# An encoder block on one core: the first head pair's bias and values loaded in the value stage, and value weights' low parts made on VectorE

## The chip, the cores and the metric

The kernel runs on one core of one Trainium2 chip. The metric is the device time of one execution in microseconds (us). Engines are called as the profile calls them: PE (TensorE, matrix products; PEld is its weight load), DVE (VectorE), ACT (ScalarE), POOL (GpSimd), and SP (SyncE), whose queue issues the transfers between HBM and the on-chip memory. PSUM is the memory into which PE writes, in eight banks.

## The reference

One layer of an encoder over 1024 positions of width 1024, all in float32. A conditioning vector gives six rows (shift, scale and gate for two halves); what matters here is the first half:

```
ada = silu(c) @ w_ada + b_ada          # six rows of 1024
h   = RMSNorm(x) * (1 + scale1) + shift1
[qA|kA|vA|qB|kB|vB|gA|gB] = h @ w_in   # widths 512 x 6, 1024 x 2
A: dilated window attention, patterns (128,1), (512,4), (2048,16) on the same q, k, v,
   merged per position by their softmax denominators, with a relative bias; 8 heads of 64
B: 2-D neighbourhood attention, 8 x 16 window, learned bias; 8 heads of 64
m = sigmoid(gA)*(oA @ w_branch_dil) + sigmoid(gB)*(oB @ w_branch_na);  x += gate1 * (m @ w_out)
```

After that come the feed-forward half (up projection, depthwise convolution, gated product, down projection) and a last norm, which the change doesn't touch.

## The kernel before, in words

Every product is done in a split form: an operand is copied by ACT to a rounded high part (`hi`), the rest (`lo`) is formed by a subtraction on POOL or DVE (`split`, line 54), and three matmuls hi*hi, hi*lo, lo*hi are summed in PSUM (`product`, line 74).

*The opening* (lines 385 to 460) takes the first 512 positions (x[0]). While its squares are summed, `warm` (line 207) keeps PE going with products of the identity into the PSUM tile `first`. Then follow four quarters q: `piece_bias` takes a quarter of shift and scale, `modulate` makes h for two of eight k tiles (DVE, ACT, DVE, by the two PSUM staging tiles `pcol` and `first`), PE adds them to the first q and k products and to the value products `pv`, and DVE sums the rows of `w_ada` for the next quarter (`ada_rows`, line 157), which PE then sums over partitions (`ada_sums`, tile `pada`). In the last quarter the second pair of value weights is loaded and split, with both low parts on POOL (line 424); the tile set is `vwh`, `vwl`. The squares of the second half of positions are divided over the quarters 2 and 3.

*The value stage* (lines 480 to 505, and 530) makes 24 value products `v_product` of 24 matmuls each, into three PSUM tiles `pv`. For each, `v_out` (line 244) lets ACT copy the result into a staging tile `vs`, of which there are three, and SP stores it to HBM (`vas`, `vbc`). Beside them run DVE's row sums over `wada` tiles (`row_pairs`), seven loads ahead, and copies from HBM to HBM which put the values in the order of the attention's blocks (`va_chunks`, and later `vb_chunks` for branch B).

*The attention of branch A* (`attend_dil`, line 555) starts with three things that come from HBM: the mask `lnm` (line 772, once), the bias `bt` of each head (lines 563 and 564; POOL adds the mask to its second part, line 565), and the values of the head, four transfers by `va_load` inside `v_tile` (lines 507 and 520), which ACT and POOL then split. For each of four residues r, PE makes scores into one of two tiles `S`, DVE adds the bias and takes the minimum (line 575), ACT takes the exponential, PE transposes, ACT and DVE split, and PE multiplies with the values into `O`.

*Order and memory.* Up to line 506 the order of the instructions on each engine is as written (`manual_schedule`). Everything after is put in order by a planner which works with a model of times, and it can put later instructions into gaps of the written order: the first score tile of head 0 and the second pair's q products are done among the value products. Pools are taken from a stack; `sm_pool`, which holds mask, bias, values and softmax tiles, is taken after `work` (the value weights and staging tiles, `adapool` and `early` (the `wada` tiles, row sums and squares) are released, and lies over their memory. A tile waits until what lay in its place was last read.

The lines that carry the two spots:

```
            if q == 3:
                v_w.append(v_split(v_load(0, 1), (pool, pool)))      # 424
    ...
            if q == 2:
                accs = sq_accs()
                square(x[1], accs, range(3), dve)                    # 435
    ...
        vs = work.tile([128, 256], FT, name="vs", bufs=3)            # 245
        act.activation(vs, p, AF.Copy)
```

Of the kernel before, what the change touches and what calls it, by code (L numbers as in the profile page):

```python
# [28 lines left out]
def hybrid_encoder(tc, xT, c, w_ada, small, w_in, p1_bias, p23_bias, na_bias, ln2_mult, ident, w_br, w_out,  # L29
# [8 lines left out]
    def f(ap):  # L38
        return ap.bitcast(FT)
# [73 lines left out]
    adapool = tc.alloc_tile_pool(name="ada", bufs=1, reuse_waits="tile")  # L113
    work = tc.alloc_tile_pool(name="start", bufs=2, reuse_waits="tile")
    ps_n = tc.alloc_tile_pool(name="psn", bufs=1, space=PSUM, reuse_waits="tile")
# [128 lines left out]
    def v_out(br, hv, st, p):  # L244
        vs = work.tile([128, 256], FT, name="vs", bufs=3)
        act.activation(vs, p, AF.Copy)  # L246
        sp.dma_start((va_s, vb_c)[br][st * 128:st * 128 + 128, hv * 256:hv * 256 + 256], vs)

    sig = work.tile([128, KT], FT, name="sig", bufs=1)
    act.activation(sig, cs, AF.Sigmoid)  # L250
# [134 lines left out]
    with tc.manual_schedule(engines={e.engine for e in (sp, act, dve, pool, pe)}):  # L385
# [29 lines left out]
        ada_sums([(wt[0][0], ones)], pa)  # L415
        warm(4, first[:, :128], True)
        stage[0] = ps_n.tile([128, 512], FT, name="pcol")
# [3 lines left out]
        for q in range(4):  # L421
            ks = range(2 * q, 2 * q + 2)
            if q == 3:
                v_w.append(v_split(v_load(0, 1), (pool, pool)))
            piece_bias(q, pa)
            modulate(x[0], 0, ks, pb)
            qk_products(ks)
            if q < 3:
                ada_rows(wt[q + 1], range(6))
            if q == 0:  # L430
                qk_split(1, (dve, dve))
                v_split(v_raw, (dve, dve), slice(4, 8), v_w[0])
            if q == 2:
                accs = sq_accs()
                square(x[1], accs, range(3), dve)
            if q == 3:
                square(x[1], accs, range(3, 8), dve)
            v_products(0, (0, 1), ks)
            if q < 3:
                pa = ada_sums([(wt[q + 1][t], cs[:, t:t + 1]) for t in (6, 7)], stop=False)  # L440
                ada_sums([(wt[q + 1][0], ones)], pa)
            v_products(0, (2, 3), ks)
# [23 lines left out]
        def row_pairs(n0, n1):  # L466
            for n in range(n0, n1):
# [9 lines left out]
                if n + 7 < len(pairs):  # L477
                    rows[n + 7] = pair_load(*pairs[n + 7])

        for n, (br, hv, st) in enumerate(v_steps[:19]):  # L480
            if n == 4:
# [20 lines left out]
            if n == 17:  # L502
                act.activation(sig, cs, AF.Exp)
            if n == 18:
                ada_bias(36, ada_sums([(sums.pop(9), ones)]))
        dve.scalar_tensor_tensor(am2, ada[:, 32:40], 1.0, g_ffn, OP.add, OP.mult)
    def va_load(head, vr):
        cc = slice(64 * head, 64 * head + 64)
        sp.dma_start(vr[:, 0:8], va_s.rearrange("(t p) n -> p t n", p=128)[:, :, cc])
        sp.dma_start(vr[:, 8:15], va_b[1:8].rearrange("j p n -> p j n")[:, :, cc])  # L510
        for x_, j in ((0, 0), (64, 8)):
            sp.dma_start(vr[x_:x_ + 64, 15], va_b[j, 0:64, cc])

# [5 lines left out]

    def v_tile(load, head, parts):  # L520

        vv = sm_pool.tile([128, 16, 128], FR, name="vv")
        lo = vv[:, :, 64:128]
        load(head, f(lo))
        for m, cs_ in parts:
            act.activation(vv[:m, cs_, 0:64], f(lo[:m, cs_]), AF.Copy)  # L526
            pool.tensor_tensor(lo[:m, cs_], f(lo[:m, cs_]), f(vv[:m, cs_, 0:64]), OP.subtract)  # L527
        return vv
# [3 lines left out]
    work.release()  # L532
    adapool.release()
    early.release()
    ps_s.release()
# [3 lines left out]
    ps_a = tc.alloc_tile_pool(name="psa", bufs=2, space=PSUM, reuse_waits="tile")  # L539
    sm_pool = tc.alloc_tile_pool(name="sm", bufs=2, reuse_waits="tile")  # L540

# [13 lines left out]
    def attend_dil(pr, qk, work):  # L555
# [3 lines left out]
        for i in range(2):  # L559
            head = 2 * pr + i  # L560
            a = slice(64 * i, 64 * i + 64)
            bt = sm_pool.tile([128, 896], FT, name="bias", bufs=2)
            sp.dma_start(bt[:, 0:512], p1_bias[head])
            sp.dma_start(bt[:, 512:896], p23_bias[head])
            pool.tensor_tensor(bt[:, 512:896], bt[:, 512:896], lnm, OP.add)
            vv = v_tile(va_load, head, ((128, slice(0, 16)),))

# [127 lines left out]
    def attend_na(pr, qk, work):  # L695
        qs, ks, kl, qb = qk
        oT = work.tile([128, S], FT, name="u1")
        for i in range(2):
# [3 lines left out]
            st = work.tile([128, 2, 8], FT, name="stb")  # L702
            vv = v_tile(vb_load, head, ((96, slice(0, 4)), (128, slice(4, 12)), (96, slice(12, 16))))
            col = 0
# [65 lines left out]
    with tc.tile_pool(name="at", bufs=2, reuse_waits="tile") as work:  # L770
        lnm = sm_pool.tile([128, 384], FT, name="lnm", bufs=1)
        sp.dma_start(lnm, ln2_mult)
# [685 lines left out]
```

## Time and profile before

| | |
|---|---|
| runs | 1565.9, 1569.3, 1570.37 us; median 1569.3 |
| profiled execution | 1566.2 us, of which the span of its instructions is 1564.4 us |
| PE busy | 1509.5 us, 96% of the span |
| DVE, ACT, POOL busy | 1024.4, 805.8, 801.8 us |
| granted clock of PE, mean | 0.982 of full speed |
| opening, value stage, first head pair | about 0 to 62, 62 to 174 and 174 to 260 us |

A row of a timeline has the start in us from the span's start, the duration in us, the engine, the line of the kernel, the operation, output <- input with partitions x elements, how many such instructions follow one another, and in brackets the idle time of the engine before and what ended it. SPq is the queue of SP; the time of a transfer there is that of its issue, not of its landing. A row of waits has the waiting engine, tile and line, what it waited for, then the total in us, the number of times and the longest. A row of stretches has its bounds, its length, the busy time (and count) of PE, PEld, DVE, ACT and POOL, the clock granted to PE (1.00 is full speed), the share of the DMA engines and GB/s.

### The profile page before, as it was taken

The numbers are of one execution on the slowest core, as the hardware profiler recorded it, in microseconds if no ns is written. First come the engines' busy times: TensorE is split into PE (matmuls) and PEld (weight loads), VectorE is DVE, ScalarE is ACT, GpSimd is POOL, SyncE is SP. The second block draws the span as 40 slices with busy tenths as digits, with TensorE's granted clock in tenths as the row PEclk, the third lists the DMA queues.
The fourth block names the chain that finished last, engine by engine and source line by source line (L and its number), as shares of the span: only waits on it lengthen the run. The fifth ranks groups of instructions, "written<-read, shape, count | busy, mean of one in ns | idle before, by whom it ended". The sixth has DMA issues, their size and how long they took to land. (4 is left out here: it accounts for less than half of the span.)

```text
span 1564.4 us, 22094 instructions
## 1 busy us (share of the span) xinstructions
PE 1509.5 (96%) x8012; PEld 1291.5 (83%) x8012; DVE 1024.4 (65%) x1874; ACT 805.8 (52%) x1448; POOL 801.8 (51%) x500
## 2 busy tenths in 40 slices
PE   8999799999999999999999888999999999999998
PEld 7899788888887998888888767888888887788787
DVE  6686266676756665535625888766666667877775
ACT  4432366666766677643335454444444446575542
POOL 1242243444337566411256858666666665679621
PEclk9899899999999999999999999999999999999999
DMA  9458522223133453557734212322222223533313
GB/s 352 164 201 292 156 73 73 81 77 93 51 90 111 141 138 104 184 187 238 228 128 149 74 54 81 108 81 81 81 82 90 86 74 136 182 114 121 115 54 109
DMA packets 114421, 196.87 MB, mean 126 GB/s; under 512 B 40200, under 2 KB 61576, under 8 KB 114312
## 3 DMA queue, kind: packets, MB, share of 16 engines
q1 hardware_dynamic: 114040, 195.20, 38.0%
q8 instruction: 63, 1.03, 0.3%
q14 instruction: 46, 0.38, 0.1%
q10 hardware_dynamic: 272, 0.26, 0.1%
HBM read 158.73 MB, written 42.47 MB: 129 GB/s over the span
## 5 line engine op out<-in xcount | busy, mean ns | idle before, releaser
L56 POOL TENSOR_TENSOR wlo<-wraw,whi 128x1024 fp32r<-128x1024 f32 (+2 forms) x78 | 179.9, 2307 | 284.1 <-ACT whi L55 275.1
L79 PE MATMUL pj<-h,whi 128*128 128x512 f32 x448 | 180.5, 403 | 3.8 <-ACT h L202 2.2
L80 PE MATMUL pj<-h,whi 128*128 128x512 f32 x448 | 179.4, 400 | 0.3 <-DVE h L204 0.3
L81 PE MATMUL pj<-h,wlo 128*128 128x512 f32 x448 | 178.8, 399 | 0.0
L56 POOL TENSOR_TENSOR wsl<-big,wsh 128x1024 fp32r<-128x1024 f32 (+1 forms) x45 | 109.3, 2432 | 50.6 <-ACT wsh L55 50.6
L1144 DVE SCALAR_TENSOR_TENSOR big<-wc,sm,big 128x256 f32<-128x256 f32 (+1 forms) x132 | 115.0, 919 | 17.3 <-ACT big L1138 17.2
L55 ACT ACTIVATE whi<-wraw 128x1024 fp32r<-128x1024 f32 (+2 forms) x81 | 81.3, 1003 | 87.0 <-PE pj L80 25.9
L338 POOL TENSOR_SCALAR kl<-kl 64x512 fp32r<-64x512 f32 x32 | 63.8, 1994 | 80.4 <-DVE kl L336 78.1
L79 PEld LDWEIGHTS pj<-h,whi 128*128 128x128 f32 x448 | 85.3, 190 | 20.6 <-ACT ks L337 3.4
L80 PEld LDWEIGHTS pj<-h,whi 128*128 128x128 f32 x448 | 85.4, 191 | 15.9 <-DVE h L204 1.1
L81 PEld LDWEIGHTS pj<-h,wlo 128*128 128x128 f32 x448 | 85.2, 190 | 15.0
L575 DVE CUSTOM_DVE_ANT_0 P<-S,bias 128x256 f32<-128x256 f32 x128 | 52.3, 420 | 53.7 <-PE S L622 31.9
L576 ACT ACTIVATE P<-P,st 128x256 f32<-128x256 f32 x128 | 64.3, 503 | 39.3 <-DVE st L575 38.7
L1144 DVE SCALAR_TENSOR_TENSOR big<-pj,sm,big 128x512 f32<-128x512 f32 x132 | 67.9, 564 | 16.1 <-ACT big L1138 16.1
L56 POOL TENSOR_TENSOR wsl<-wraw,wsh 128x768 fp32r<-128x768 f32 (+1 forms) x23 | 50.1, 2178 | 47.7 <-ACT wsh L55 47.7
L1138 ACT ACTIVATE big<-wc,sm 128x512 f32<-128x512 f32 x44 | 35.8, 816 | 74.5 <-DVE wc L961 45.6
L239 PE MATMUL pv<-vwh,h 128*128 128x256 f32 x256 | 73.7, 288 | 0.4 <-ACT vs L246 0.4
L240 PE MATMUL pv<-vwl,h 128*128 128x256 f32 x256 | 72.5, 283 | 0.0
L241 PE MATMUL pv<-vwh,h 128*128 128x256 f32 x256 | 72.5, 283 | 0.0
L527 POOL TENSOR_TENSOR vv<-vv 96x256 fp32r<-96x256 f32 (+2 forms) x32 | 41.0, 1294 | 59.3 <-ACT vv L526 59.1
L55 ACT ACTIVATE wsh<-big 128x1024 fp32r<-128x1024 f32 (+1 forms) x45 | 44.9, 1002 | 35.4 <-POOL big L913 18.3
L1170 ACT ACTIVATE big<-big 128x1024 f32<-128x1024 f32 x22 | 23.3, 1060 | 76.6 <-DVE big L1144 76.6
(379 smaller groups left out, 4923.7 us busy)
## 6 DMA issues: line engine op xcount, KB each, us to landing
wraw<-w_in SPq DMA_DIRECT2D x36, 512.0 KB, 3.5
wada<-w_ada SPq DMA_DIRECT2D x31, 512.0 KB, 7.1
big<-w_up SPq DMA_DIRECT2D x22, 512.0 KB, 5.0
wraw<-w_up SPq DMA_DIRECT2D x22, 512.0 KB, 3.7
as<-big SPq DMA_DIRECT2D x22, 512.0 KB, 3.0
big<-as SPq DMA_DIRECT2D x22, 512.0 KB, 8.1
wraw<-w_down SPq DMA_DIRECT2D x24, 384.0 KB, 4.2
gs<-gs SPq DMA_DIRECT2D x32, 256.0 KB, 2.5
```

The lines of the kernel that those rows point to most:

```text
L55: act.activation(hi, raw, AF.Copy)
L56: lo_eng.tensor_tensor(lo, raw, f(hi), OP.subtract)
L79: pe.matmul(psum, whi[:, k0 + k], mhi, start=k == 0, stop=False)
L80: pe.matmul(psum, whi[:, k0 + k], mlo, start=False, stop=False)
L81: pe.matmul(psum, wlo[:, k0 + k], mhi, start=False, stop=k == n - 1)
L239: pe.matmul(p, hhi, hi[:, k], start=fresh and k == 0, stop=False, skip_group_check=True)
L240: pe.matmul(p, hhi, lo[:, k], start=False, stop=False, skip_group_check=True)
L241: pe.matmul(p, hlo, hi[:, k], start=False, stop=k == KT - 1, skip_group_check=True)
L338: pool.tensor_scalar(ll[b], f(ll[a]), 1.0, None, OP.mult)
L575: dve.tensor_tensor_reduce(pp, d, bias, -1.0, BIG, OP.add, OP.min, mi)
L576: act.activation(pp, pp, AF.Exp, bias=mi, scale=-1.0, accum_out=li)
L1144: dve.scalar_tensor_tensor(y[:, dst], src, wt, y[:, dst], OP.mult, OP.add)
```

## The change

The mask, and bias and values of heads 0 and 1, are loaded at the end of the written order, behind the store of the nineteenth value product and ahead of the last five, by `dil_loads`; `attend_dil` takes these (`loads.pop(0)`), and calls `dil_loads` itself for later heads. `v_tile` no longer loads. For that `sm_pool` is taken earlier, over `adapool` and `early` only; `work` is moved to the other side of the memory, `vs` has two tiles and not three, and the small tile `sig` becomes one of the weight pool's `rs` tiles. In the opening the second value weights are loaded and split in quarter 2, with both low parts on DVE, after DVE's row sums of that quarter; all eight squares of the second half come in quarter 3; and the third `warm` has twelve products and not four.

```
-    work = tc.alloc_tile_pool(name="start", bufs=2, reuse_waits="tile")
+    work = tc.alloc_tile_pool(name="start", bufs=2, side="right", reuse_waits="tile")
...
-        vs = work.tile([128, 256], FT, name="vs", bufs=3)
+        vs = work.tile([128, 256], FT, name="vs", bufs=2)
...
-    sig = work.tile([128, KT], FT, name="sig", bufs=1)
+    sig = wpool.tile([128, KT], FT, name="rs", bufs=2)
...
-        warm(4, first[:, :128], True)
+        warm(12, first[:, :128], True)
...
-            if q == 3:
-                v_w.append(v_split(v_load(0, 1), (pool, pool)))
+            if q == 2:
+                v_raw1 = v_load(0, 1)
             piece_bias(q, pa)
             modulate(x[0], 0, ks, pb)
             qk_products(ks)
...
             if q == 2:
+                v_w.append(v_split(v_raw1, (dve, dve)))
+            if q == 3:
                 accs = sq_accs()
-                square(x[1], accs, range(3), dve)
-            if q == 3:
-                square(x[1], accs, range(3, 8), dve)
+                square(x[1], accs, range(8), dve)
...
+        def v_raw(load, head):
+            vv = sm_pool.tile([128, 16, 128], FR, name="vv")
+            load(head, f(vv[:, :, 64:128]))
+            return vv
+
+        def dil_loads(head):
+
+            bt = sm_pool.tile([128, 896], FT, name="bias", bufs=2)
+            sp.dma_start(bt[:, 0:512], p1_bias[head])
+            sp.dma_start(bt[:, 512:896], p23_bias[head])
+            return bt, v_raw(va_load, head)
...
-                act.activation(sig, cs, AF.Exp)
+                act.activation(wpool.tile([128, KT], FT, name="rs", bufs=2), cs, AF.Exp)
...
+        adapool.release()
+        early.release()
+        sm_pool = tc.alloc_tile_pool(name="sm", bufs=2, reuse_waits="tile")
+        lnm = sm_pool.tile([128, 384], FT, name="lnm", bufs=1)
+        sp.dma_start(lnm, ln2_mult)
+        loads = [dil_loads(head) for head in range(2)]
...
     for br, hv, st in v_steps[19:]:
         v_out(br, hv, st, v_product(st, v_w[br, hv]))
     work.release()
-    adapool.release()
-    early.release()
...
-            bt = sm_pool.tile([128, 896], FT, name="bias", bufs=2)
-            sp.dma_start(bt[:, 0:512], p1_bias[head])
-            sp.dma_start(bt[:, 512:896], p23_bias[head])
+            bt, vv = loads.pop(0) if loads else dil_loads(head)
             pool.tensor_tensor(bt[:, 512:896], bt[:, 512:896], lnm, OP.add)
-            vv = v_tile(va_load, head, ((128, slice(0, 16)),))
+            vv = v_tile(vv, ((128, slice(0, 16)),))
...
-        lnm = sm_pool.tile([128, 384], FT, name="lnm", bufs=1)
-        sp.dma_start(lnm, ln2_mult)
```

More of the change, by code (lines that the diff above doesn't have):

```diff
@@ L478, in row_pairs, with va_load @@
                     rows[n + 7] = pair_load(*pairs[n + 7])
+        def va_load(head, vr):
+            cc = slice(64 * head, 64 * head + 64)
+            sp.dma_start(vr[:, 0:8], va_s.rearrange("(t p) n -> p t n", p=128)[:, :, cc])
+            sp.dma_start(vr[:, 8:15], va_b[1:8].rearrange("j p n -> p j n")[:, :, cc])
+            for x_, j in ((0, 0), (64, 8)):
+                sp.dma_start(vr[x_:x_ + 64, 15], va_b[j, 0:64, cc])
+        def v_raw(load, head):
[7 more added lines that the diff above has]
+            return bt, v_raw(va_load, head)
         for n, (br, hv, st) in enumerate(v_steps[:19]):
@@ L506, in hybrid_encoder @@
         dve.scalar_tensor_tensor(am2, ada[:, 32:40], 1.0, g_ffn, OP.add, OP.mult)
[L507 to L512, printed above, removed]
+        adapool.release()
[4 more added lines that the diff above has]
+        loads = [dil_loads(head) for head in range(2)]
     def vb_load(head, vr):
@@ L518, in vb_load, with v_tile @@
             sp.dma_start(vr[:16 * n, 4 * cb:4 * cb + 4], vb_s[cb].rearrange("(g p) n -> p g n", g=4)[:, :, cc])
-    def v_tile(load, head, parts):
-        vv = sm_pool.tile([128, 16, 128], FR, name="vv")
+    def v_tile(vv, parts):
         lo = vv[:, :, 64:128]
-        load(head, f(lo))
         for m, cs_ in parts:
@@ L539, in hybrid_encoder @@
     ps_a = tc.alloc_tile_pool(name="psa", bufs=2, space=PSUM, reuse_waits="tile")
-    sm_pool = tc.alloc_tile_pool(name="sm", bufs=2, reuse_waits="tile")
     def finish_o(po, dst):
@@ L702, in attend_na @@
             st = work.tile([128, 2, 8], FT, name="stb")
-            vv = v_tile(vb_load, head, ((96, slice(0, 4)), (128, slice(4, 12)), (96, slice(12, 16))))
+            vv = v_tile(v_raw(vb_load, head), ((96, slice(0, 4)), (128, slice(4, 12)), (96, slice(12, 16))))
             col = 0
```

## The prediction

> **What bounds it now.** I read the busy table and then the waits of TensorE, over the whole span (total, times, longest).
>
> ```profile
> PE 1509.5 (96%) x8012; PEld 1291.5 (83%) x8012; DVE 1024.4 (65%) x1874; ACT 805.8 (52%) x1448; POOL 801.8 (51%) x500
> ```
>
> ```profile
> PE S L591 <- DVE st L575: 7.6, 1, 7.6
> PE pbc L106 <- DVE rs L100: 5.1, 2, 4.3
> PE pj L949 <- DVE T1lo L895: 3.0, 1, 3.0
> PE pada L148 <- DVE wada L164: 2.9, 1, 2.9
> ```
>
> TensorE (PE) is busy 96% of the span, so what can be won is its idle time and its slow clock. Its longest single wait, 7.6 us, is at the first attention scores; 2.9 us more are lost in the opening at the conditioning sums. The change touches exactly the code around these two. The stretches before, in and after the first wait (PE and its clock are the columns to read; the others are PEld, DVE, ACT, POOL, then DMA), and then the timeline of that place:
>
> ```profile
> 165.00:173.40 8.40, 8.40 (x56) 7.37 (x54) 0.00 (x0) 0.83 (x3) 0.00 (x0) 1.00 0.39 119
> 173.40:181.00 7.60, 0.07 (x1) 0.00 (x0) 1.10 (x4) 1.47 (x2) 3.33 (x2) 0.80 0.86 215
> 181.00:190.50 9.50, 8.20 (x44) 7.37 (x44) 5.36 (x22) 8.07 (x22) 5.71 (x3) 0.62 0.77 207
> ```
>
> ```profile
> 154.27 0.95 PE L148 MATMUL pada<-ones,sq 128*128 128x1 f32 x8
> 157.81 0.53 SPq L247 DMA_DIRECT2D vbc<-vs  x1
> ...
> 173.51 0.53 SPq L247 DMA_DIRECT2D vbc<-vs  x1
> 174.14 0.38 SPq L772 DMA_DIRECT2D lnm<-ln_mult  x1
> 179.56 0.99 POOL L565 TENSOR_TENSOR bias<-bias,lnm 128x384 f32<-128x384 f32 x1 [2.75 <-DMA bias<-p_bias]
> 180.59 0.42 DVE L575 CUSTOM_DVE_ANT_0 P<-S,bias 128x256 f32<-128x256 f32 x1 [5.00 <-POOL bias L565]
> 181.07 0.58 PE L591 MATMUL S<-ks,qs 128*128 128x256 f32 x1 [7.60 <-DVE st L575]
> 181.90 1.06 ACT L526 ACTIVATE vv<-vv 128x1024 fp32r<-128x1024 f32 x1 [7.03 <-DMA vv<-vab]
> ```
>
> The chain is plain: head 0's mask and bias are issued only at 174.1, behind the last store of values; they land at 179.56, GpSimd adds, VectorE takes the scores, and PE gets a free score tile at 181.07. Its clock, 1.00 before, is 0.62 until 190.5. The memory of these tiles lies over pools of the conditioning stage, last read near 155.2 (the sums at 154.27), and over the value stage's own pool, which the change moves to the other side.
>
> **The change part by part.**
>
> *The early loads.* Nothing is added: the mask, and six transfers a head, move from 174.14 to the end of the written order, behind the nineteenth store (157.81). Head 0's bias was there at 179.56 and its values at 181.90, 5.4 and 7.8 us after the first issue. From 158.4 that makes 163.8 and 166.2, or 170.9 and 173.3 if all wait the 7.1 us more that a loaded queue shows below; PE now has work without them until 173.4. So the 7.6 us go. Behind it, 8.20 busy us at a clock of 0.62 are 5.1 at full rate: up to 9.5 - 5.1 = 4.4 us lie in the stretch to 190.5. The chain score, softmax, transpose, product is still there for the first tiles, so I take 2.5 of them (bounds 0 and 4.4): -10.1 us. What was hidden: SP now issues thirteen transfers, at some 0.5 us, 6.5 us in all, ahead of the last five stores and of the copies of the other branch's values. Those copies are wanted four head pairs later and cost nothing; the stores hold a staging tile, and I put 0.5 us on them (0 to 3: three products can run on in PSUM).
>
> *VectorE takes the low parts.* The opening's third quarter:
>
> ```profile
> 47.00 5.16 POOL L56 TENSOR_TENSOR vwl<-wraw,vwh 128x1024 fp32r<-128x1024 f32 x2 [23.53 <-ACT vwh L55]
> 35.94 3.90 DVE L164 SCALAR_TENSOR_TENSOR wada<-wada,cs 128x512 f32<-128x512 f32 x5
> 45.63 4.33 DVE L164 SCALAR_TENSOR_TENSOR wada<-wada,cs 128x512 f32<-128x512 f32 x3
> 50.00 3.50 DVE L164 SCALAR_TENSOR_TENSOR wada<-qb,cs,wada 128x512 f32<-128x512 f32 x2
> 53.42 1.48 DVE L182 TENSOR_TENSOR sq<-sq,mt 128x512 f32<-128x512 f32 x2
> 53.55 1.86 PE L148 MATMUL pada<-ones,wada 128*128 128x1 f32 x8 [2.94 <-DVE wada L164]
> 55.46 0.16 DVE L255 TENSOR_TENSOR ada<-pada,sm 128x4 f32<-128x4 f32 x1 [0.56 <-PE pada L148]
> 56.64 0.69 ACT L202 ACTIVATE h<-pcol,ada 128x512 fp32r<-128x512 f32 x1 [8.77 <-DVE pcol L201]
> 57.99 0.61 PE L79 MATMUL pj<-h,whi 128*128 128x512 f32 x1
> 59.58 2.29 DVE L182 TENSOR_TENSOR sq<-sq,mt 128x512 f32<-128x512 f32 x3 [0.21 <-ACT mt L180]
> 66.60 1.84 PE L93 MATMUL pcol<-ones,sq 128*128 128x1 f32 x16
> L56 DVE TENSOR_TENSOR wlo<-big,whi x1: 1225/1225/1225, 873.4 to 873.4; 128x1024 fp32r<-128x1024 f32 x1
> ```
>
> While GpSimd makes the two low parts (47.0 to 52.2), VectorE's five row sums take 4.33 + 3.50; the five of the quarter before, with GpSimd idle, took 3.90. So 3.9 us are lost beside GpSimd, and with it idle they end at 45.63 + 3.90 = 49.5. PE was done with its earlier products at 53.55 - 2.94 = 50.6, so its wait is gone; its eight need some 1.0 (half of the sixteen at 66.60) and end near 51.7. VectorE's two low parts cost 2 x 1.225 and end at 52.0; the bias that waited until 55.46 comes at 52.0. PE's twelve value products (53.55 + 1.86 to 57.99 now, 2.7 with its slow clock) run from 51.7 to 54.4, and the first h (56.64 + 0.69, so 1.9 us after the bias at 55.46) is there at 53.9. So 57.99 becomes 54.4: -3.6 us. Bounds: -2.0 if the moved weights land or are copied late (GpSimd starts on them at 47.0 now, so their copies are in time for 49.5), -4.6 with a warm clock. On SP the second value weights keep their place, since nothing is issued between the old and the new spot. The two square additions (1.48 us) move behind the next products; the squares end at 61.87 now and the sums on PE start at 66.60, so cover is 4.7 us: nothing, and 1.5 us if it were gone.
>
> *Twelve warming products.* The first quarter:
>
> ```profile
> 19.68 1.14 PE L210 MATMUL pv<-idt 128*128 128x128 f32 x8
> 21.73 0.75 DVE L201 SCALAR_TENSOR_TENSOR pv<-h,am,pbc 128x512 f32<-128x512 f32 x1
> 23.00:27.00 4.00, 4.00 (x10) 2.84 (x10) 3.86 (x7) 0.94 (x3) 0.47 (x1) 0.50 1.04 395
> 32.20 0.16 DVE L255 TENSOR_TENSOR ada<-pada,sm 128x4 f32<-128x4 f32 x1 [1.46 <-PE pada L148]
> ```
>
> Each is two matmuls, so sixteen come on top of eight that took 1.14: 2.3 us, to 23.1. They write the PSUM tile that VectorE's second modulation (21.73) also writes, so that may start 1.4 us later. VectorE has 1.46 us of slack at 32.20, which covers it. PE's clock was 0.50 from 23 to 27, ten matmuls; at best that half is saved. I take 0, bounds -1.5 and +1.0. On this the Trainium skill ("TensorE: Matmul & The Clock Gate", "What's actually happening") says that the clock opens after a busy window of some 3.4 us; by that rule, with 20.8 (19.68 + 1.14) to 24.2 filled it would open one window earlier and the sum would be some 1.6 us lower, an estimate from that page. By that rule the trace agrees, in that the clock was at half after a stretch with PE partly idle; no run here has the window filled.
>
> *Two staging tiles for the stores, not three.* This speaks against the change.
>
> ```profile
> DMA to landing us min/median/max: 6.7/7.1/7.5
> 118.10 0.39 ACT L246 ACTIVATE vs<-pv 128x256 f32<-128x256 f32 x1 [2.11 <-DMA vas<-vs]
> 125.12 0.38 ACT L246 ACTIVATE vs<-pv 128x256 f32<-128x256 f32 x1 [6.63 <-DMA vas<-vs]
> 125.56 0.38 PE L239 MATMUL pv<-vwh,h 128*128 128x256 f32 x1 [0.36 <-ACT vs L246]
> 132.39 0.40 PE L80 MATMUL pj<-h,whi 128*128 128x512 f32 x1
> 132.62 0.40 PE L79 MATMUL pj<-h,whi 128*128 128x512 f32 x1
> 161.02 0.39 ACT L246 ACTIVATE vs<-pv 128x256 f32<-128x256 f32 x1 [2.42 <-PE pv L241]
> ```
>
> (The first row is of the staging tile.) A store lands 7.1 us after its issue, and ScalarE already waits for the third store back. With two tiles it waits for the second: the copy of 118.10 moves to the landing that released 125.12. A product takes 2.42 + 0.39 = 2.8 us (161.02) and waits for the copy three before it. The one before 125.56 ended at 125.2, so it began at 122.4; it could now not begin before that copy ends at 125.5: 3.1 us of PE. Later ones meet the next pair's projections, 96 matmuls 0.23 apart (132.39 to 132.62), 22 us that PE can do meanwhile. I take +3.0; bounds 0 (the queue, not the tile, may be what is late) and 10 (no projections in the gaps: of the same lag at the three or so later places where ScalarE waits).
>
> The sigmoid in another pool's tile, and the pool's side, add no instruction: 0.
>
> **Sum.** -10.1 + 0.5 - 3.6 + 0 + 3.0 = -10.2 us. The profiled execution took 1566.2 us, so 1556.0 for its like; that execution lies 3.1 us under the median of the runs (1569.3, from 1565.9), which less 10.2 is 1559.1. I predict **1558**.
>
> **Rivals.**
>
> *The staging tiles decide (slower).* Two tiles pass one store per (7.1 + 0.4 copy + 0.4 issue) / 2 = 3.95 us where a product takes 2.8. Over the 19 products from the sixth on that is 21.9 us. If PE has nothing ordered into these gaps, 1566.2 - 13.7 + 0.5 + 21.9 = 1575. It decides from a loss of 13.2 us, that is 0.7 us a product or a landing of 6.2 us throughout. For it: all the waits shown above; against: PE itself lost only 0.36 us to these waits so far, and it has 22 us of projections to fill with. 0.11.
>
> *The loads stay late.* The planner may put copies ahead of them, or they crawl behind the queue's load, and land near 180 as now; then only the opening is won: 1566.2 - 3.6 + 3.0 = 1566. For it: the queue is in order, and its stores run to 173.5; against: their place in the order is written, and their memory was last read at 155.2. 0.14.
>
> *Everything overlaps.* Scores and softmax of head 0 go under the last products, all 4.4 us come, the clock opens early, the staging costs nothing: 1566.2 - 12.0 - 4.6 - 1.5 = 1548. For it: VectorE is idle and ScalarE busy 0.83 us in 165.00 to 173.40, so there is room for the softmax. 0.12.
>
> *A wait in its place, later.* The orders of all engines after the opening are planned anew from a model of times, so waits like the 4.3 us at a norm or the 3.0 at a stage change (second and third row of the waits) can come or go: some 4 us either way on every case, held by the range.
>
> **How the numbers follow.** The forecast, with its own range of 1553 to 1564, has 0.63; its neighbours 0.11, 0.14, 0.12 as above. About 0.3%, 4.7 us, is what a measurement here can tell from none: faster is under 1564.6, slower over 1574.0. Faster: 0.61 of the forecast, 0.12 and 0.03 of the late loads, 0.76; slower: 0.09 of the staging rival; the same: 0.02 of it, 0.11 of the late loads and 0.02 of the forecast, 0.15. The range, 1548 to 1570, leaves out about one in ten at each end (the bounds above add up to 1566.2 - 18.1 and 1566.2 + 4.4).
>
> **What would show it.** Early loads: issues of mask and bias before 160, no PE wait for the softmax near 170, clock 1.00 there. VectorE: no L164 above 0.8 us, the wait of 2.9 gone, the fourth quarter's products near 54.4. Staging: ScalarE's waits for stores grow, and PE waits for L246 copies by 3 us. Wrong it would be if those waits passed 13 us, or the 7.6 us came back under another name in the first head pair.

## The result

| | before | after |
|---|---|---|
| median of six runs each | 1569.49 us (1565.9 to 1573.73) | 1561.01 us (1556.99 to 1562.4) |
| profiled execution, and its span | 1566.2, 1564.4 us | 1562.4, 1560.6 us |

The ratio is 0.994, 95% interval 0.9924 to 0.9955: 8.5 us faster by the medians. Run again later beside other kernels, the changed kernel had 0.994 once more (0.9919 to 0.996). The forecast of 1558 in a range of 1548 to 1570 holds the time. The two profiled executions lie only 3.8 us apart, because that of before was 3.3 us under its median and that of after 1.4 over; what follows by place is for that pair.

TensorE's waits over the span of the changed kernel (total, times, longest; L603 and L587 are the scores and the maximum that stood at L591 and L575, L610 and L588 the transposes and the exponential that stood at L598 and L576):

```profile
PE pv L239 <- ACT vs L246: 4.0, 2, 3.5
...
PE S L603 <- DVE st L587: 2.6, 5, 0.7
...
PE T L610 <- ACT P L588: 1.9, 1, 1.9
```

The 7.6 us at the first scores and the 2.9 us at the conditioning sums are gone. New are 4.0 us at the value products, which wait for ScalarE's copies into the staging tiles, five short waits at scores, and 1.9 us at the first transposes. The stretches, before and then after (bounds, length, busy time and count of PE, PEld, DVE, ACT, POOL, PE's clock, DMA share, GB/s):

```profile
110.00:145.00 35.00, 34.59 (x275) 33.30 (x275) 26.61 (x33) 6.71 (x11) 10.59 (x4) 1.00 0.88 322
145.00:180.00 35.00, 28.47 (x219) 26.98 (x217) 4.90 (x10) 7.47 (x15) 2.78 (x2) 0.97 0.64 187
180.00:200.00 20.00, 17.70 (x94) 15.52 (x95) 11.22 (x36) 14.18 (x38) 7.57 (x5) 0.80 0.39 102
410.00:482.00 72.00, 66.45 (x428) 59.57 (x426) 46.85 (x133) 48.63 (x109) 28.95 (x19) 1.00 0.28 79
```

```profile
110.00:145.00 35.00, 30.95 (x210) 29.48 (x209) 19.16 (x25) 7.30 (x12) 9.89 (x4) 0.90 0.88 310
145.00:180.00 35.00, 35.00 (x284) 34.44 (x283) 10.75 (x25) 7.53 (x17) 4.38 (x3) 1.00 0.69 198
180.00:200.00 20.00, 17.53 (x95) 15.81 (x94) 10.05 (x31) 13.66 (x40) 4.90 (x3) 0.83 0.41 116
250.00:300.00 50.00, 48.11 (x283) 42.50 (x282) 31.41 (x94) 35.62 (x85) 21.74 (x15) 0.97 0.24 68
410.00:482.00 72.00, 71.36 (x457) 63.96 (x456) 49.72 (x147) 51.31 (x118) 29.39 (x19) 1.00 0.31 92
```

What TensorE loses in a stretch is its length less busy time times clock. From 110 to 145 us that was 35 - 34.59 = 0.4 and is 35 - 30.95 x 0.90 = 7.1: 6.7 us worse. From 145 to 180 it was 35 - 28.47 x 0.97 = 7.4 and is 0. From 180 to 200 it was 20 - 17.70 x 0.80 = 5.8 and is 20 - 17.53 x 0.83 = 5.5. From 250 to 300, where the second head pair begins, it was 0.1 (49.86 us busy at full clock) and is 50 - 48.11 x 0.97 = 3.3, a loss that the prediction's sum doesn't have. From 410 to 482 it was 5.5 and is 0.6. This last place is one that neither the change nor the prediction touches: the hand-over from the last head pair of branch A to the first of B. The stores of the two branches' results mark how far the kernels are, before and then after (SP's issues, shortest, median and longest in ns, first and last start in us):

```profile
L693 SPq DMA_DIRECT2D oa<-u x4: 337/338/423, 263.8 to 481.3; - x4
L758 SPq DMA_DIRECT2D ob<-u x4: 319/332/338, 537.4 to 691.4; - x4
```

```profile
L705 SPq DMA_DIRECT2D oa<-u x4: 326/337/338, 265.8 to 481.4; - x4
L770 SPq DMA_DIRECT2D ob<-u x4: 320/357/430, 535.8 to 684.3; - x4
```

At the first store of branch A (263.8 and 265.8) the changed kernel is 2.0 us *behind*, about what the places up to there add up to: -0.6 in the opening (below), +6.7, -7.4, -0.3 and +3.3 make +1.7. At A's last store it is level (481.3, 481.4), and at B's last 7.1 us ahead (691.4, 684.3), of which 3.8 are left at the end of the span. So in this pair the places that the prediction summed bring nothing by themselves. The result came out near the forecast, but not by its sum, and the experiments have to say why.

**The opening.** VectorE and TensorE of the changed kernel, in order of time:

```profile
19.86 4.55 PE L210 MATMUL pv<-idt 128*128 128x128 f32 x24
24.45 0.76 DVE L201 SCALAR_TENSOR_TENSOR pv<-h,am,pbc 128x512 f32<-128x512 f32 x1 [2.61 <-PE pv L210]
44.99 0.17 DVE L255 TENSOR_TENSOR ada<-pada,sm 128x4 f32<-128x4 f32 x1 [3.98 <-PE pada L148]
48.73 2.33 DVE L164 SCALAR_TENSOR_TENSOR wada<-wada,cs 128x512 f32<-128x512 f32 x3
51.10 1.54 DVE L164 SCALAR_TENSOR_TENSOR wada<-qb,cs,wada 128x512 f32<-128x512 f32 x2
52.55 2.35 DVE L56 TENSOR_TENSOR vwl<-wraw,vwh 128x1024 fp32r<-128x1024 f32 x2
54.83 0.15 DVE L255 TENSOR_TENSOR ada<-pada,sm 128x4 f32<-128x4 f32 x1
```

With GpSimd idle the five row sums take 2.33 + 1.54 = 3.9 us and the two low parts 2.35, as worked out. From the third bias to the fourth it is 54.83 - 44.99 = 9.8 us; before it was 55.46 - 41.89 = 13.6. But the third bias itself is 3.1 us later than before, so the fourth is only 0.6 us earlier. The twenty-four warming matmuls took 4.55 us and VectorE's modulation waited 2.61 us for them, yet at the second bias only 1.2 us of the delay are there (33.37 for 32.20). The other 1.9 come behind it, where TensorE ran at half clock from 33.7 to 40.5 us. The kernel with its stores on ScalarE's queue (below) has the same 4.55 us and not this second stretch, and its third bias is at 42.44.

**The staging tiles.** ScalarE, SP's queue and TensorE of the changed kernel, the landing times of those two stores between 100 and 128 us for which the profile tells one (shortest, median, longest), and a stretch behind the wait:

```profile
105.49 0.39 ACT L246 ACTIVATE vs<-pv 128x256 f32<-128x256 f32 x1 [0.63 <-DMA vas<-vs]
106.72 3.14 SPq L60 DMA_DIRECT2D wraw<-w_in  x2
110.42 0.38 SPq L247 DMA_DIRECT2D vas<-vs  x1
112.61 4.47 SPq L374 DMA_DIRECT2D vab<-vas  x4
115.33 0.39 ACT L246 ACTIVATE vs<-pv 128x256 f32<-128x256 f32 x1 [7.86 <-DMA vas<-vs]
119.67 0.36 SPq L247 DMA_DIRECT2D vas<-vs  x1
126.47 0.38 ACT L246 ACTIVATE vs<-pv 128x256 f32<-128x256 f32 x1 [5.10 <-DMA vas<-vs]
126.91 0.58 PE L239 MATMUL pv<-vwh,h 128*128 128x256 f32 x1 [3.45 <-ACT vs L246]
```

```profile
DMA to landing us min/median/max: 6.7/6.9/7.1
```

```profile
130.00:132.00 2.00, 2.00 (x12) 2.00 (x11) 0.00 (x0) 1.36 (x2) 1.62 (x1) 0.50 1.02 328
```

The wait is at the place that the prediction named, 3.45 us for 3.1. Behind it TensorE ran at half clock until about 132 us, some 2.5 us more, which the prediction had left out. And the reason is not the landing alone. The copy of 105.49 ended at 105.9, and its store was issued at 110.42, behind the weight loads in SP's queue that the row of 106.72 begins. It gave its tile back for the copy of 115.33, whose own store was issued only at 119.67, some 4 us after its end, behind the copies from HBM to HBM that the row of 112.61 begins. That store took 6.7 us to land, and the copy of 126.47 waited for it.

**The early loads.** The same kernel at the first scores:

```profile
164.38 0.53 SPq L247 DMA_DIRECT2D vbc<-vs  x1
165.01 0.38 SPq L530 DMA_DIRECT2D lnm<-ln_mult  x1
167.51 0.39 ACT L246 ACTIVATE vs<-pv 128x256 f32<-128x256 f32 x1 [3.38 <-PE pv L241]
172.57 0.42 DVE L587 CUSTOM_DVE_ANT_0 P<-S,bias 128x256 f32<-128x256 f32 x1 [7.72 <-POOL bias L577]
175.77 1.00 SPq L247 DMA_DIRECT2D vbc<-vs  x2
178.98 1.06 ACT L543 ACTIVATE vv<-vv 128x1024 fp32r<-128x1024 f32 x1 [3.62 <-DMA vv<-vab]
182.94 0.39 ACT L246 ACTIVATE vs<-pv 128x256 f32<-128x256 f32 x1 [2.36 <-DMA vbc<-vs]
183.87 1.52 PE L610 MATMUL T<-idt,P 128*128 128x128 f32 x6 [1.91 <-ACT P L588]
```

The loads start at 165.01, not 174.14, and VectorE takes the first scores at 172.57, not 180.59: TensorE no longer waits for them. But the copy of 167.51 is stored only at 175.77, 7.9 us after its end, behind the thirteen early transfers. With the 2.1 to 3.1 us that stores take to land here, its tile is back at about 178 to 179. Until 178.98 ScalarE also stands 3.62 us for another reason, the load of head 1's values, which it splits before it copies again (at 179.95). The store of that copy goes out at once, at 180.33, but with two tiles ScalarE stands 2.36 us for it before the copy of 182.94. The exponential is behind that copy in ScalarE's queue, and the transposes wait 1.91 us for it. Which of the two held ScalarE more, the late store or the late values, these rows don't show.

### The profile page after: what moved, and what is told of

It reads as the page before. It is cut to its first block, busy times and chain, and to the rows that moved or that the text cites. A ratio compares the mean times of both kernels' runs of the same rounds, so it can differ in the third digit from the quotient of the medians.

```text
span 1560.6 us, 22134 instructions
## 1 busy us (share of the span) xinstructions
PE 1509.3 (97%) x8028; PEld 1298.1 (83%) x8028; DVE 1017.4 (65%) x1876; ACT 804.1 (52%) x1448; POOL 795.0 (51%) x498
## 4 chain that ended last, share of the span: by engine, by line
PE 72%; DVE 11%; POOL 5%; DMA 4%; ACT 4%; issue 3%; SPq 1%; DVEq 0%; POOLq 0%; ACTq 0%
PE pj L79 10%; PE pj L80 10%; PE pj L81 10%; PE pj L960 9%; PE pj L959 9%; PE pj L958 9%; DVE big L1154 2%; PE pj L311 2%; DMA wraw<-w_down 2%; PE O L762 2%; POOL wsl L56 1%; DVE sq L476 1%; PE T L750 1%; PE O L617 1%; PE pv L239 1%
## 5 line engine op out<-in xcount | busy, mean ns | idle before, releaser
L587 DVE CUSTOM_DVE_ANT_0 P<-S,bias 128x256 f32<-128x256 f32 x128 | 51.9, 420 | 70.7 <-PE S L634 43.3
L588 ACT ACTIVATE P<-P,st 128x256 f32<-128x256 f32 x128 | 64.3, 504 | 47.5 <-DVE st L587 46.9
L239 PE MATMUL pv<-vwh,h 128*128 128x256 f32 x256 | 75.3, 294 | 4.0 <-ACT vs L246 4.0
L241 PE MATMUL pv<-vwh,h 128*128 128x256 f32 x256 | 74.2, 290 | 0.0
L740 POOL TENSOR_SCALAR P<-P,stb 128x288 f32<-128x288 f32 (+1 forms) x32 | 39.2, 1226 | 52.1 <-DVE stb L737 42.3
```

What stands on the lines that cost most here:

```text
L239: pe.matmul(p, hhi, hi[:, k], start=fresh and k == 0, stop=False, skip_group_check=True)
L241: pe.matmul(p, hlo, hi[:, k], start=False, stop=k == KT - 1, skip_group_check=True)
```

## The experiments

Ratios are to the kernel before on the same chip, with 95% intervals; a thousandth is 1.57 us. Four parts of the change were taken alone or away first, then three points were tested: the number of warming products, the early loads without the opening's part, and the queue that issues the stores. The early loads with three staging tiles weren't run, since the third tile's place is given to them; what it would have saved is not measured.

### One part alone on the kernel before

The part on VectorE:

```
-            if q == 3:
-                v_w.append(v_split(v_load(0, 1), (pool, pool)))
+            if q == 2:
+                v_raw1 = v_load(0, 1)
...
             if q == 2:
+                v_w.append(v_split(v_raw1, (dve, dve)))
+            if q == 3:
                 accs = sq_accs()
-                square(x[1], accs, range(3), dve)
-            if q == 3:
-                square(x[1], accs, range(3, 8), dve)
+                square(x[1], accs, range(8), dve)
```

> The kernel before with only the opening's second value weights moved to quarter 2 and their low parts on VectorE (squares in quarter 3 as in the change). Theory: row sums free of GpSimd, the PE wait of 2.9 us gone, the bias of the fourth quarter 3.6 us earlier (51.9 and not 55.5): 1569.5 - 3.6 = 1566 us, ratio 0.9977. Rival: the value stage is bound by its stores and loads, so the gain is given back before the attention: 1569 us, ratio 1.000, with PE or ScalarE waits for stores grown by 3 us.

Measured: 1566.03 us, 0.9989 (0.9977 to 1.0), or 1.7 us less, with 3.6 at the edge of the interval. In its profile the wait for the row sums is gone and the fourth bias stands at 52.45 us, 3.0 before that of the kernel before. TensorE's instructions are in the order of the kernel before up to 1341 us, so this run measures little but the part: 0 to 3.6 us.

The twelve warming products:

```
-        warm(4, first[:, :128], True)
+        warm(12, first[:, :128], True)
```

> The kernel before with only the third warming raised from four to twelve products. Theory: VectorE's second modulation waits 2.6 us for PE, and 1.2 us at the second quarter and 3.1 us at the third remain: 1569.5 + 3 = 1572.5 us, ratio 1.002. Rival (the prediction's step): VectorE's slack of 1.46 us covers it: 1569.5 us, ratio 1.000, bias of the third quarter at 41.9 us as before.

Measured: 1566.66 us, 0.9996 (0.9984 to 1.0007). The interval holds the term of 0, but TensorE's order differs from that of the kernel before from 189 to 558 us, so this run doesn't isolate the products. In its profile the twenty-four matmuls took 2.92 us, not 4.55, and the third bias is at 40.97 us, 0.9 before that of the kernel before.

The two staging tiles:

```
-        vs = work.tile([128, 256], FT, name="vs", bufs=3)
+        vs = work.tile([128, 256], FT, name="vs", bufs=2)
```

> The kernel before with only two staging tiles for the stores of values and not three. Theory: one PE wait of 3.1 to 3.5 us near 122 to 126 us for the copy of three products before, and after it a clock of 0.50 for one or two windows (some 3 us): 1569.5 + 6.5 = 1576 us, ratio 1.004. Rival (the prediction's term): 3 us, ratio 1.002, since projections fill the rest and the clock stays up. Second rival: nothing, the early transfers of the change are what delays the stores there.

Measured: 1565.8 us, 0.9983 (0.9969 to 0.9997): not slower, though the wait is there:

```profile
126.45 0.49 PE L239 MATMUL pv<-vwh,h 128*128 128x256 f32 x1 [3.42 <-ACT vs L246]
```

From 110 to 145 us TensorE loses 5.7 us in this kernel, 5.3 more than before; from 410 to 482 us it loses 0.7, 4.8 less. So a tile fewer changes what the planner does 300 us later, and the profile has there about what the tile costs. An experiment that changes one size here changes two things.

### The changed kernel with four warming products

```
-        warm(12, first[:, :128], True)
+        warm(4, first[:, :128], True)
```

> The changed kernel with four warming products again and not twelve. Theory: the sixteen more matmuls ran at half clock (24 in 4.55 us) and held VectorE's second modulation of the first quarter by 2.6 us; the second quarter's and third quarter's bias came 1.2 and 3.1 us later than in the kernel before. Without them the opening ends 3 us earlier: 1561 - 3 = 1558 us, a ratio of 0.9925 to the kernel before, and the bias of the fourth quarter comes near 51.7 us, not 54.8. Rival: the warming keeps the clock up for what follows; then the time is 1561 or more, and the clock in 20 to 40 us lies below the 0.76 of the changed kernel.

Measured: 1567.41 us, 0.9997 (0.9982 to 1.0012). Without the eight further products the whole gain is gone, though on the kernel before they showed none. Either they are worth 6 us in this kernel, or they decide something else. The instruction lists point to the second: TensorE's first 1400 rows are the same, but the attention of the kernel with twelve is ordered otherwise than with four, and the kernel with four has a long stretch of it, the hand-over within, as the kernel before has it. At the hand-over it has the two waits of before (total, times, longest, from 410 to 482 us):

```profile
PE S L729 <- DVE stb L733: 2.7, 1, 2.7
PE O L617 <- ACT th L592: 2.3, 1, 2.3
```

### Six and ten products: the order or the products

Six and ten products give the same order as twelve up to the end of the attention.

```
-        warm(12, first[:, :128], True)
+        warm(6, first[:, :128], True)
```

> The changed kernel once more, unaltered, to stand beside the three below on the same chip. Both theories: 0.994 of the kernel before, 0.992 to 0.997 (about 1559 us where the kernel before takes 1568).

> The changed kernel with 6 warming products instead of 12 (4 gave 0.9997 of before, 12 gave 0.994). Of the attention and the hand-over between its branches it has the instruction order of the changed kernel, not that of the one with 4. Theory 'order': the 6 us between 4 and 12 come from the order that the planner makes of the attention, so 6 goes with 12: 0.993 to 0.996, and the stretch from 410 to 482 us loses under 1.5 us of TensorE time. Theory 'warming': they come from the clock that the products keep up in the opening, so 6 goes with 4: 0.998 to 1.001, and the first quarter's bias sums end later than in the changed kernel.

> The changed kernel with 10 warming products; the order up to the end of the attention is that of 6 and of 12 (0.9925 and 0.994), not that of 4 (0.9997). Theory 'order': 0.992 to 0.996, with no wait of TensorE over 1.5 us from 410 to 482. Rival 'warming': a value between that of 6 and that of 12 would fit both, so it falls to this run only if it comes out at 0.998 or over, or if the opening's bias sums end over 1 us earlier than with 4.

Measured: with twelve 1560.83 us, 0.994 (0.9919 to 0.996); with six 1557.97 us, 0.9925 (0.9909 to 0.994); with ten 1559.8 us, 0.9939 (0.9922 to 0.9957). Two more products than four bring all of it, and six more than that nothing. The stretch of the hand-over in the kernel with six (with four TensorE was busy 66.42 us of it, at full clock):

```profile
410.00:482.00 72.00, 71.36 (x451) 63.52 (x449) 49.84 (x142) 49.58 (x114) 32.30 (x21) 1.00 0.31 92
```

5.6 us are lost there with four and 0.6 with six. The times follow the order and not the number. What isn't shown is that these 5 us alone make the difference of the medians. In the profiled executions the last store of branch B starts at 691.4 us with four products and at 681.4 with six, but at the ends of the spans (1561.8 and 1556.6) only 5.2 of these 10.0 us are left, and the profiled execution with four was the fastest of its twelve runs.

### Early loads without the part on VectorE

The changed kernel, with the opening as before and four warming products:

```
-        warm(12, first[:, :128], True)
+        warm(4, first[:, :128], True)
...
-            if q == 2:
-                v_raw1 = v_load(0, 1)
+            if q == 3:
+                v_w.append(v_split(v_load(0, 1), (pool, pool)))
```

> The early loads and the two staging tiles, without the VectorE part of the opening and with 4 warming products. The prediction's terms give -10.1 +0.5 +3.0 = -6.6 us, 0.996 of before (0.993 to 0.998). Theory 'order': its hand-over between the branches is ordered as in the changed kernel, so 0.994 to 0.997, with the 5 us of 410 to 482 gone. Rival 'the early loads buy nothing by themselves, the wait only moves': 0.999 to 1.002.

Measured: 1570.11 us, 1.0012 (1.0 to 1.0025). Both the prediction's terms (-6.6 us) and the theory of the order fail here, and the rival holds: as they stand, with two staging tiles, the early loads gain nothing. In the profile the 7.6 us are gone, but one wait of 2.6 us at the first transposes and one of 3.8 at the staging tiles are there, and at A's first store (266.4 us) it is 2.6 us behind the kernel before.

This kernel has the smoother hand-over too (1.7 us lost from 410 to 482), and gives that back from 482 to 700 and 880 to 940 us (6.7 and 14.2 us lost, 3.4 and 12.7 before). So a good hand-over is not enough for a gain. Up to 264 us TensorE has the order of the changed kernel here, so the 2.6 us at A's first store are the cleaner reading; from there to 481 us the order is another one.

### The stores on ScalarE's queue

If the stores are late because they stand behind loads in SP's queue, another queue should mend both new waits. With four warming products:

```
-        sp.dma_start((va_s, vb_c)[br][st * 128:st * 128 + 128, hv * 256:hv * 256 + 256], vs)
+        act.dma_start((va_s, vb_c)[br][st * 128:st * 128 + 128, hv * 256:hv * 256 + 256], vs)
```

> The changed kernel with 4 warming products, and each store of a values' tile issued from ScalarE's queue right behind the copy that fills the tile, not from SP's. Theory 'the store stands in SP's queue behind the early loads, and that is what ScalarE and then TensorE wait for': the wait of 3.5 us near 126 us and the half clock after it go, and the time is 3 to 6 us under that of the kernel with 4 (0.996 to 0.998 of before). Rival 'the store lands late because of the transfers themselves': the waits stay, 0.999 to 1.002.

Measured: 1547.39 us, 0.9863 (0.9845 to 0.9881): 21.6 us under the kernel before and 13.4 under the changed one, far more than expected. The stretches, and two copies, each with its store:

```profile
110.00:145.00 35.00, 35.00 (x255) 33.28 (x256) 22.33 (x30) 6.69 (x11) 10.35 (x4) 1.00 0.86 307
145.00:180.00 35.00, 33.40 (x258) 32.49 (x257) 10.68 (x34) 16.23 (x41) 9.12 (x5) 0.95 0.77 221
180.00:200.00 20.00, 20.00 (x122) 17.72 (x121) 10.85 (x28) 13.91 (x33) 10.52 (x9) 1.00 0.13 35
```

```profile
106.68 0.38 ACT L246 ACTIVATE vs<-pv 128x256 f32<-128x256 f32 x1 [2.50 <-PE pv L241]
107.09 0.33 ACTq L247 DMA_DIRECT2D vas<-vs  x1
126.60 0.37 ACT L246 ACTIVATE vs<-pv 128x256 f32<-128x256 f32 x1
135.19 0.33 ACTq L247 DMA_DIRECT2D vbc<-vs  x1
```

Up to 114 us a store now follows its copy by 0.03 us. Four between 116 and 137 us still stand 2.7 to 8.2 us in ScalarE's queue (that of the copy of 126.60 the longest) and hold ScalarE, but TensorE has other products meanwhile. TensorE loses nothing from 110 to 145 us (7.1 in the changed kernel), 35 - 33.40 x 0.95 = 3.3 from 145 to 180 and nothing from 180 to 200. Up to 131 us TensorE's order is that of the kernel with four products and the stores on SP, so the wait at the staging tiles came from SP's queue. The other new wait stays: the transposes still wait 1.5 us for the exponential, as they do with the stores on SP (1.6). The Trainium skill ("DMA: Bandwidth & Descriptors", "Issuing engines are not separate DMA queues") says that issuing from several engines saves only the issue time, which it calls usually small. Here the measurement decides: the store of one copy was issued 4.5 us after it in SP's queue, and that of another 7.9 us. From 145 to 200 us this kernel loses 3.3 us where the kernel before loses 13.2: 9.9 us, which is what the prediction's early loads should have brought (-10.1 + 0.5). The early loads are issued from 159.33 us here, not from 165.01. From 131 to 690 us the order is another one, so the whole difference isn't the queue's alone. But of the 15.9 us between the spans of these two profiled executions (1561.8 and 1545.9), 12.4 are there at A's first store (262.4 and 250.0), so most of it was won by then.

The same edit on the whole change, on the early loads alone, and on the kernel before:

> The whole change (12 warming products), with the stores of the values' tiles issued from ScalarE's queue. TensorE's order is that of the same kernel with 4 warming products up to the end of the attention, so the two differ by the products alone there. The prediction's term: 0, bounds -1.5 and +1.0 us: 1546 to 1549, 0.985 to 0.988 of before. Rival 'the products themselves bring the 6 us that lay between 4 and 12': about 1541, 0.982. Rival 'they cost what they delay': 1550, 0.988 to 0.990.

> The early loads, two staging tiles and stores from ScalarE's queue, with the opening as before: without the part on VectorE and with 4 warming products. TensorE's order is the same, product for product, as in the kernel with the VectorE part (0.9863 of before, 1547.4 us), so the difference is that part alone. The prediction's term: 3.6 us (bounds 2.0 and 4.6), so 1551, 0.988 to 0.990. Rival 'what is won in the opening is lost again behind it' (as the 0.9989 of the part alone on the kernel before could mean): 1547 to 1548, 0.986 to 0.987.

> The kernel before with nothing but the stores issued from ScalarE's queue; three staging tiles, late loads. Theory 'the late landing hurts only with two tiles and with loads between the stores': TensorE lost 0.4 us to staging before, so 0.997 to 1.001, and the wait of 7.6 us at the first scores stays. Rival 'the stores' place in SP's queue cost the kernel before as much': that wait becomes shorter by the time that the last stores land sooner, and 0.990 to 0.995.

Measured: the whole change with stores on ScalarE 1551.58 us, 0.9882 (0.9864 to 0.99). Twelve products are 0.0019 over four (on another chip), with some 0.0025 of uncertainty (both half-widths, squared and added): -1 to +7 us. The order is the same in both up to the end of the attention. That they bring 6 us is out; whether they cost 3 is not told apart from 0.

The early loads without the part on VectorE: 1553.66 us, 0.99 (0.9884 to 0.9916). TensorE's instructions are in the same order as with that part, so this is a clean pair, though its two kernels ran on two chips, each against the kernel before on its own: 0.0037 with some 0.0024 of uncertainty, 2 to 10 us, for the part on VectorE. The prediction's 3.6 lies in it, and "lost again behind it" doesn't. On one chip this kernel and the whole change with the same stores (0.9882) are 0.0018 apart, with 0.0024 of uncertainty, but those two differ by the products as well. Its fourth bias:

```profile
56.86 0.16 DVE L255 TENSOR_TENSOR ada<-pada,sm 128x4 f32<-128x4 f32 x1 [0.56 <-PE pada L148]
```

The row sums are back at 4.34 + 3.51 us beside GpSimd, and the fourth bias is at 56.86 us where the kernel with the part has it at 51.85. Of these 5.0 us, 1.3 were there at the third bias already (43.28 and 42.02), as this execution's clock in the opening was lower.

The kernel before with the new queue alone: 1565.01 us, 0.9972 (0.9958 to 0.9985), 4.4 us. Its profiled execution was the slowest of its runs, so only single rows are read from it:

```profile
117.92 0.39 ACT L246 ACTIVATE vs<-pv 128x256 f32<-128x256 f32 x1 [2.42 <-PE pv L241]
123.23 0.33 ACTq L247 DMA_DIRECT2D vbc<-vs  x1
123.66 0.38 ACT L246 ACTIVATE vs<-pv 128x256 f32<-128x256 f32 x1 [5.35 <-DMA wada<-w_ada]
```

Here a store on ScalarE's queue was issued 4.9 us after its copy, held by a load of `wada` as the profile puts it, and ScalarE stood behind it. So the other queue is no cure by itself: without the early loads the kernel gains 4 us, and from 132 to 687 us TensorE's order is not that of the kernel before, so even these aren't the queue's alone. Beside this kernel the one with early loads and two tiles (0.99) is lower by another 0.0072 (with some 0.0021 of uncertainty), 8 to 15 us, where the sum without a staging loss says 9.6; here, too, the orders differ. Which part of the 21.6 us is the order that the planner made for these kernels isn't known; TensorE loses 1.3 us from 410 to 482 in the best one.

## Why the prediction was right or wrong

*The time* was right: 1561.0 for 1558, inside the range and inside the likeliest case's own range of 1553 to 1564. *The sum behind it* was right for VectorE's part and wrong in what the tiles and the early loads cost and bring, so that the time fell so near is luck. The kernel with four warming products shows it. It has every other part of the change, the sum gives the same 1558 for it (the products are a term of 0), and from 275 us to the end of the attention its order is that of the kernel before. It gained nothing (0.9997, at most 2.8 us by its interval, where the sum says 10). In its profile the fourth bias is 3.5 us earlier than before (52.00). TensorE loses 35 - 31.39 x 0.95 = 5.2 us from 110 to 145 (4.8 more than before), 1.6 from 145 to 180 (5.8 less), 20 - 18.58 x 0.83 = 4.6 from 180 to 200 (1.2 less), and 50 - 48.03 x 0.97 = 3.4 from 250 to 300 (3.3 more). That is -2.4 us, and its span is 2.6 us shorter (1561.8 for 1564.4). So the early loads brought 7.0 us for 9.6, the tiles cost 4.8 for 3.0, and 3.3 were lost at the second head pair, where the sum has nothing.

*VectorE takes the low parts, -3.6:* right. The quarter became 13.6 - 9.8 = 3.7 us shorter, the row sums took 3.9 us, and with four products the fourth quarter's first product comes at 54.15 us where 54.4 was worked out (57.99 before; 57.20 in the changed kernel, whose third bias is late). The two runs whose order is kept give 0 to 3.6 and 2 to 10 us.

*Twelve warming products, 0 (-1.5 to +1.0):* by the medians not told apart from 0. In the profiled execution the products took 4.55 us, most of it at half clock, where 2.3 more than 1.14 were counted. The 1.46 us of slack didn't cover the wait of 2.61, and the second bias came 1.2 us later; of the 3.1 at the third, the rest is the later stretch of half clock. The Trainium skill's rule ("TensorE: Matmul & The Clock Gate", "What's actually happening"), by which a filled window opens the clock, agrees in part: in the changed kernel the clock was full at 26 us, but it was at half again from 33.7 to 40.5.

*Two staging tiles, +3.0 (0 to 10):* right in place and mechanism, too small. The wait was 3.45 us where 3.1 were worked out, one more of 0.59 came at 119.5, and the half clock behind it wasn't in the sum; 6.7 us in all, inside the bounds. The step that failed is to price the wait alone and put the clock behind it at nothing. And "a store lands 7.1 us after its issue" is only part of a tile's way: the stores ahead of this wait first stood some 4 to 4.5 us in SP's queue. The trace of the kernel before had this already: its copy of 109.48 was stored at 118.31, 8.4 us after its end.

*The early loads, -10.1 + 0.5:* half right. The 7.6 us went, though the issues began at 165.01 and not 158.4 (the nineteenth store itself had moved from 157.81 to 164.38, about the 6.7 us that the staging tiles cost); the margin held it. The term that failed is "I put 0.5 us on them", for the stores behind the thirteen transfers. The first one was 7.9 us late and the load of head 1's values held ScalarE until about the same time. The wait behind them (1.91 us) came at the very first transposes, so that the 2.5 us of cold stretch, too, were not won: 5.5 us are lost from 180 to 200 where it was 5.8. The bound of 3 us was drawn from three products running on in PSUM; it didn't see that ScalarE's exponentials stand behind its copies and its splits of the values in the same queue. With the stores elsewhere the full 9.9 us are there, though 1.5 us of that wait remain.

*Later waits, "some 4 us either way":* this term, which the forecast put at 0, decided the result. At A's first store the profiled execution was 2.0 us behind, and the gain came behind it, 4.9 us of it at the hand-over of 410 to 482 us, in an order that the planner chose. The kernel with the same change but four warming products has the other order and no gain. The measured 8.5 us are therefore to a good part a different order, which the prediction had no means to foresee; its neighbour "the loads stay late" (1566, for no gain but the opening's) was nearer to the time of the kernel with four products (1567.4), though the loads are early there.

*The rival "the staging tiles decide"* (1575) was too high: TensorE lost 6.7 us to them, not the 13.2 from which it would have decided. *"Everything overlaps"* (1548) is the time that the kernel with stores on ScalarE reached, 1547.4, by an edit that the prediction doesn't have.

## What to carry to other kernels

When a transfer is moved ahead in an in-order queue, price what it pushes back there by the whole path, from the instruction that fills the buffer to its release and on to whatever else stands in that instruction's queue; here the early loads took away a wait of 7.6 us, and the staging tile given up for them cost TensorE 6.7 us. Look whether another queue can take the small urgent transfers: on top of the early loads, one changed word brought more than the change itself. Where a planner orders the rest, compare the instruction orders before believing an experiment: four warming matmuls more moved the ratio from 0.9997 (four products of two) to 0.9925 (six), some 11 us, and only a pair with equal orders measures an edit.

## What the runs showed of the hardware that was not expected

TensorE's clock in the opening differs between kernels whose written opening is the same. The changed kernel, and the same with its stores on ScalarE (whose first store is after 59 us), from 36 to 46 us:

```profile
36.00:46.00 10.00, 10.00 (x58) 8.91 (x58) 5.77 (x11) 0.00 (x0) 0.00 (x0) 0.77 1.03 387
```

```profile
36.00:46.00 10.00, 9.28 (x64) 8.24 (x63) 7.78 (x14) 1.81 (x3) 0.00 (x0) 1.00 1.02 369
```

At 0.77 of full speed 58 matmuls fill the stretch, at 1.00 it holds 64 and has room. A second profiled execution of the changed kernel has 0.79 there. In both kernels the twenty-four warming matmuls took 4.55 us, most of it at half clock; in the kernel before with twelve products twenty-four took 2.92 us, and in the kernel with ten products twenty took 2.48. What sets this isn't known from these runs. The Trainium skill ("TensorE: Matmul & The Clock Gate", "What's actually happening") says that the window by which the clock is granted runs freely and doesn't begin with the kernel. That would fit, but no run here moved a kernel against that window.

A store issued by ScalarE can hold ScalarE: 4.9 us in the kernel before with the stores on its queue, by the profile for a load of another engine's tile, and 8.2 us in the fastest kernel.
